# Folding the chunk inverse into the operand of a bidirectional RWKV-7 chain, with grams and transposes in 64x64 tiles

## The chip, the cores and the metric

The kernel runs on one core of one Trainium2 chip, as one program. The metric is the device time of one execution in microseconds, the median of three runs. A core has five engines that work from their own in-order queues: TensorE (PE; its weight loads are listed as PEld), VectorE (DVE), ScalarE (ACT), GpSimd (POOL) and SyncE (SP), which here only issues DMAs.

## The reference: what is computed

Two layers of a token mixer run over 256 context tokens and 1024 latent tokens of width 1024. Each layer projects its input once, and the columns go to three groups of heads: A, a bidirectional RWKV-7 recurrence (6 heads of 64); B, grouped-query attention; C, neighbourhood attention on a grid. Each group is gated, all are concatenated, projected and normalised. The change lies in A, whose recurrence is, for each token and each direction:

```
def _rwkv7_step(S, inp):
    r, w, k, v, kk, b = inp
    sa = einsum('bhvk,bhk->bhv', S, kk)
    S = S * w[:, :, None, :] - sa[..., None] * b[:, :, None, :] + v[..., None] * k[:, :, None, :]
    return S, einsum('bhvk,bhk->bhv', S, r)
```

The state S is 64x64 per head. It is carried from the context into the latent tokens, once forwards and once backwards, and the two outputs are added.

## The kernel before, in words

`layer_proj` (L182) makes the projections. Its last part and the whole of `attention` (L831: the heads of B and C, two PSUM banks for `st`, two for `sm`, one for `y`) are written after the recurrent part `rwkv` (L516) but run beside it: the program is built under a planner (`schedule_with_timeline_sim=True`), which puts each engine's instructions in an order by program order and by its own estimate of when each is ready. So each queue holds a mixture of recurrent work and attention work, in a fixed order. `out_proj` (L1144) follows when attention and the recurrent part have written their gated outputs.

The recurrent part cuts the 1280 tokens into 10 waves of 128 tokens, and a wave into 4 steps of 32 tokens. Both directions (d) and the six heads (three columns c, two halves p) go together. Within a step the recurrence is a linear system in blocks of 32 tokens: the sums `sa` of all 32 tokens come from the inverse of a triangular 32x32 matrix times a right side.

A wave has these stages, each a function that gives instructions:

- `wave_pre` (L555, letter p) loads r, kk, kd and bd by DMA, makes the decays and the scaled operands. It writes `kb` (the scaled keys) and half of the operand tile `G`; L593 clears the other half of each block of G on GpSimd. There are six G tiles, two for each of three waves.
- `wave_gram` (L612, g) multiplies `kb` with G on TensorE (L620: full 128 rows, 64 columns at a time) and writes the masked products into the cleared halves of G (L625, VectorE, sixteen instructions of 64x192 per wave).
- `wave_low` (L600, l) sends the 16x16 diagonal blocks of the matrix through DRAM into a layout for inversion.
- `wave_inv` (L641, i) inverts the 16x16 blocks on VectorE (L653, L655) and sends the result through DRAM back into `di`.
- `wave_kt` (L628, k) transposes `kb` on TensorE (L635: 128x128 transposes) and copies it into the tiles `S` (L639, ScalarE, sixteen copies per wave).
- `wave_merge` (L673, m) joins the 16x16 inverses to 32x32 ones with two rounds of 32x32 products (L684). The first is masked on VectorE (L687), the second gives `tt` (L689).

`wave_chain` (L692) then runs four steps one after the other. A step has these instructions, each dependent on the one before:

- L706 loads v into the tile `X` (three X tiles in turn, `NX = 3`) and L708 clears its sa rows, on SyncE and GpSimd;
- L713: twelve products of G with X give the right side `rs` in PSUM;
- L716: ScalarE copies it to SBUF as `rsb`;
- L724: twelve 32x32 products of `tt` with `rsb` give `sa`;
- L730: four copies put `sa` into X (three on ScalarE, one on VectorE);
- L734: twelve products of S with X give the new state, which L739 (VectorE) scales into the next X.

The step's output products (`out_step`, L754, tile `py`) are kept back in the list `pend` and given after the next step's L716, in the middle of its chain.

The stages are called in the order "ikpglm" after each wave's chain: stages i, k and m for the wave two ahead, p, g and l for the wave three ahead. `behind` (L550) holds two places of the later work behind an instruction of the chain. All PSUM tiles of the stages (psz, pcu, gt, kt, mg, py, pso) take turns in one pair of banks, the tag "pp" of the pool `pa` (L523, `bufs=2`); the chain has a bank of its own, `ch`.

## Time and profile before

| what | value |
|---|---|
| median of three runs | 2471.63 us (2459.14 to 2474.3) |
| the profiled execution, its time | 2478.63 us |
| its span in the trace | 2476.9 us, 57781 instructions |
| mean granted TensorE clock | 0.937 |
| DMA | 298.17 MB, mean 120 GB/s |

How to read the lines shown in the prediction. In a group line stand the line of the code, engine, operation, tile written and tiles read (out<-in), shapes and types with the count of records; then the busy time in microseconds and the mean of one in nanoseconds; then the idle time of the engine just before, and what ended it. For TensorE the tiling stands as rows*columns of the weights. An f32 product gives two records, a transpose one. A tile view gives minimum, median and maximum duration in ns and the start of the first and last record. In a timeline stand start and length in us and, with xN, how many like instructions are merged in the line. In the view by stretches stand for each stretch its length, busy time and count for PE, PEld, DVE, ACT and POOL, then the granted clock, the share of DMA and GB/s; restricted to one line of code, only its engines are listed. A busy PE is not a PE at its peak: the time that a product needs to run through the array is counted as busy.

### The profile page before, as it was taken

How to read it: one execution, taken by the hardware profiler on the slowest of the kernel's cores; microseconds unless marked ns; L12 is line 12 of the kernel's file. 1: busy time of each engine (PE TensorE's matmuls, PEld its weight loads, DVE VectorE, ACT ScalarE, POOL GpSimd, SP SyncE). 2: the span in 40 equal slices, each digit the busy share in tenths (PEclk: the TensorE clock that was granted, in tenths of full speed). 3: DMA queues.
4: the chain of work that ended last, by engine and by line, in shares of the span. 5: the costliest groups of instructions: out<-in, count | busy, mean ns of one | idle time of the engine just before them, and what ended most of it. 6: DMA issues, size and time to landing. Idle time of an engine off the chain costs nothing.

```text
span 2476.9 us, 57781 instructions
## 1 busy us (share of the span) xinstructions
PE 2189.6 (88%) x22616; PEld 1645.0 (66%) x22616; DVE 1625.1 (66%) x3063; ACT 1003.5 (41%) x2186; POOL 1184.1 (48%) x1438
## 2 busy tenths in 40 slices
PE   6989999987888888989899999899868788989697
PEld 3777898765555555545897777787645555556397
DVE  5686423545768777775396785525468688778646
ACT  3333413334445454463233434223345444445522
POOL 4464426335555554462245456434456545545433
PEclk9999999996879999998999999999879999999899
DMA  7344335446555444351332445334555545332522
GB/s 281 112 162 164 111 92 123 120 108 139 126 116 136 114 100 119 102 177 34 101 103 91 146 161 182 107 90 121 141 116 140 102 99 117 84 90 64 161 71 94
DMA packets 448241, 298.17 MB, mean 120 GB/s; under 512 B 249600, under 2 KB 395880, under 8 KB 446944
## 3 DMA queue, kind: packets, MB, share of 16 engines
q1 hardware_dynamic: 439936, 281.71, 41.6%
q0 software_dynamic: 7392, 10.28, 1.5%
q8 instruction: 178, 2.92, 0.5%
q10 hardware_dynamic: 640, 2.49, 0.4%
q14 instruction: 95, 0.78, 0.1%
HBM read 198.37 MB, written 91.79 MB: 117 GB/s over the span
## 4 chain that ended last, share of the span: by engine, by line
PE 44%; DVE 21%; DMA 15%; issue 7%; ACT 6%; POOL 4%; SPq 3%; DVEq 0%; POOLq 0%; ACTq 0%
PE pj L203 5%; PE pj L204 5%; PE pj L205 5%; PE y L948 4%; DMA yf<-yg_d 3%; PE st L963 3%; PE sm L894 3%; DMA ls_d<-G 3%; DVE G L625 2%; PE st L964 2%; DVE mx L896 2%; DVE tmp L653 2%; PE ch L734 2%; PE py L754 1%; DMA lin<-ls_d 1%
## 5 line engine op out<-in xcount | busy, mean ns | idle before, releaser
L204 PE MATMUL pj<-hlo,wh 128*128 128x512 f32 (+1 forms) x1072 | 401.4, 375 | 14.3 <-DVE hlo L480 8.0
L203 PE MATMUL pj<-hhi,wh 128*128 128x512 f32 (+1 forms) x1072 | 403.2, 378 | 9.4 <-ACT qr L348 5.2
L205 PE MATMUL pj<-hhi,wl 128*128 128x512 f32 (+1 forms) x1072 | 400.6, 374 | 0.2 <-POOL wl L169 0.2
L204 PEld LDWEIGHTS pj<-hlo,wh 128*128 128x128 f32 x1072 | 205.0, 191 | 56.2 <-DVE hlo L480 8.3
L203 PEld LDWEIGHTS pj<-hhi,wh 128*128 128x128 f32 x1072 | 204.4, 191 | 54.8 <-issue 6.8
L169 POOL TENSOR_TENSOR wl<-wf,wh 128x512 fp32r<-128x512 f32 x104 | 143.8, 1387 | 202.2 <-ACT wh L168 178.7
L896 DVE TENSOR_REDUCE mx<-sm 128x1 f32<-128x512 f32 (+1 forms) x372 | 198.8, 554 | 50.1 <-PE sm L894 47.6
L205 PEld LDWEIGHTS pj<-hhi,wl 128*128 128x128 f32 x1072 | 204.9, 191 | 38.4 <-issue 3.3
L970 ACT ACTIVATE pt<-st 128x512 f32<-128x512 f32 (+1 forms) x292 | 164.9, 583 | 130.1 <-PE st L964 122.8
L948 PE MATMUL y<-pt,v 128*64 128x256 f32 (+1 forms) x1392 | 211.5, 398 | 2.3 <-ACT pt L973 1.4
L894 PE MATMUL sm<-k,q 128*128 128x256 f32 (+2 forms) x436 | 166.1, 422 | 25.8 <-DVE mx L896 19.5
L963 PE MATMUL st<-q,k 128*128 128x512 f32 (+3 forms) x376 | 165.0, 444 | 21.1 <-DVE rc L1012 5.9
L1186 PE MATMUL pj<-yh,wh 128*128 128x256 f32 x576 | 160.2, 290 | 24.4 <-ACT yh L1160 23.1
L1187 PE MATMUL pj<-yl,wh 128*128 128x256 f32 x576 | 164.0, 288 | 0.8 <-POOL yl L1161 0.8
L1188 PE MATMUL pj<-yh,wl 128*128 128x256 f32 x576 | 162.2, 286 | 0.0
L977 POOL TENSOR_TENSOR acc<-acc,pt 128x512 f32<-128x512 f32 x80 | 106.4, 1330 | 102.7 <-ACT pt L970 101.4
L948 PEld LDWEIGHTS y<-pt,v 128*64 128x64 f32 x1392 | 94.0, 142 | 89.6 <-issue 58.0
L964 PE MATMUL st<-q,k 65*128 65x512 f32 (+3 forms) x376 | 146.7, 393 | 1.9 <-ACT q L908 1.2
L894 PEld LDWEIGHTS sm<-k,q 128*128 128x128 f32 x436 | 80.6, 201 | 89.8 <-DVE mx L896 37.0
L625 DVE TENSOR_TENSOR G<-gt,msk 64x192 f32<-64x192 f32 (+1 forms) x320 | 110.5, 345 | 39.7 <-PE gt L620 28.4
L708 POOL MEMSET X<- 32x192 f32 x320 | 81.2, 254 | 102.0 <-PE py L754 74.6
L1186 PEld LDWEIGHTS pj<-yh,wh 128*128 128x128 f32 x576 | 109.9, 196 | 26.0 <-ACT yh L1160 23.5
(276 smaller groups left out, 5104.5 us busy)
## 6 DMA issues: line engine op xcount, KB each, us to landing
wf<-win SPq DMA_DIRECT2D x104, 256.0 KB
wm<-wmod SPq DMA_DIRECT2D x32, 512.0 KB
yf<-yg_d SPq DMA_DIRECT2D x72, 128.0 KB
wt<-wm SPq DMA_DIRECT2D x8, 1024.0 KB
gate_d<-o SPq DMA_DIRECT2D x32, 256.0 KB
wf<-wout SPq DMA_DIRECT2D x16, 512.0 KB
ldkk<-rw_d SPq DMA_DIRECT2D x40, 192.0 KB
ldkd<-rw_d SPq DMA_DIRECT2D x40, 192.0 KB
```

The lines of the kernel that those rows point to most:

```text
L203: nc.tensor.matmul(out=ps[:, :n], lhsT=wh, rhs=hhi[:, k, t0:t0 + n], start=(k == 0), stop=False)
L204: nc.tensor.matmul(out=ps[:, :n], lhsT=wh, rhs=hlo[:, k, t0:t0 + n], start=False, stop=False)
L205: nc.tensor.matmul(out=ps[:, :n], lhsT=wl, rhs=hhi[:, k, t0:t0 + n], start=False, stop=(k == KT - 1))
L894: nc.tensor.matmul(out=sp_[:, :o], lhsT=q[0][:, qc:qc + 128], rhs=k[0][:, c0:c0 + o], start=True, stop=True)
L896: nc.vector.tensor_reduce(out=mx[:, n_:n_ + 1], in_=sp_[:, :o], op=ALU.max, axis=AX.X)
L948: mm = nc.tensor.matmul(out=y[64 * i:64 * i + 64, a0:a1], lhsT=v[:, t, :], rhs=pt[:, p0:p0 + a1 - a0], start=start, stop=stop and at == le ...
L963: nc.tensor.matmul(out=o, lhsT=k[0][:, 128 * t:128 * t + 128], rhs=q[0][:, qa:qb], start=True, stop=False)
L964: mm = nc.tensor.matmul(out=o, lhsT=k[1][0:65, 128 * t:128 * t + 128], rhs=q[1][0:65, qa:qb], start=False, stop=True)
L970: nc.scalar.activation(out=pt[:, :w], in_=sp_[:, :w], func=AF.Exp)
L1186: nc.tensor.matmul(out=p_, lhsT=wh[m][:, k], rhs=yh, start=(x_ == 0), stop=False)
L1187: nc.tensor.matmul(out=p_, lhsT=wh[m][:, k], rhs=yl, start=False, stop=False)
L1188: nc.tensor.matmul(out=p_, lhsT=wl[m][:, k], rhs=yh, start=False, stop=(x_ == KT - 1))
```

## The change

- In the chain, L716 (the copy `rsb`) and L724 (the products with `tt`) are gone; the products of L713 write `sa` directly. The output products in `pend` now stand between them and the copies into X.
- `wave_merge` keeps its first round; the mask `omk` has changed its sign, and `tt` is not made.
- A new stage `wave_fold` (letter f, called last, for the wave two ahead) finishes the inverse in PSUM by accumulation, copies it negated into a block-diagonal tile `bd`, transposes the first halves of the G operand by products with the identity, multiplies them with `bd`, and writes the result back over them. Its PSUM tiles come from the same pair of banks.
- `wave_gram` takes the two halves p as separate 64x64 products instead of one 128-row product with zeros in it, so that G needs no clearing (L593 is gone), and the masking takes eight instructions of 64x384 instead of sixteen of 64x192.
- `wave_kt` transposes by 64x64 products with the identity, and copies with eight instructions of 64x384 instead of sixteen of 64x192.

The core of the diff, without the renaming of `rs` and the sign of `omk`:

```diff
+        bd = rp.tile([128, 6, 4, 32], F32, tag="bd", name="bd")
+        nc.gpsimd.memset(bd, 0.0)
...
-                    nc.gpsimd.memset(g[64 - 64 * p:128 - 64 * p, :, :, p, 0:64 if need_r else 32], 0.0)
...
-                            nc.tensor.matmul(out=gt[64 * i:64 * i + 64, c, :, :nr], lhsT=kb[:, c, 2 * h + i, :], rhs=g[:, 2 * h + i, c, :, :nr],
-                                             start=True, stop=True, tile_position=(0, 64 * i))
+                            for p in range(2):
+                                rs_, os_ = slice(64 * p, 64 * p + 64), slice(64 - 64 * p, 128 - 64 * p)
+                                nc.tensor.matmul(out=gt[os_, i, c, :nr], lhsT=kb[rs_, c, 2 * h + i, :], rhs=g[rs_, 2 * h + i, c, p, :nr],
+                                                 start=True, stop=True, tile_position=(64 * p, 64 - 64 * p))
...
-                        nc.tensor.transpose(kt[:, c, :], kb[:, c, 2 * h:2 * h + 2, :].rearrange("q j f -> q (j f)"), ident)
+                                nc.tensor.matmul(out=kt[os_, i, c, :], lhsT=kb[rs_, c, 2 * h + i, :], rhs=ident[rs_, rs_],
+                                                 start=True, stop=True, tile_position=(64 * p, 64 - 64 * p))
...
+        def wave_fold(w):
+
+            gs, di = prep[w]["g"], prep[w]["di"]
+            for hf in range(2):
+                mg = pa.tile([128, 2, 3, 32], F32, tag="pp", name="mi")
+                for j in range(2):
+                    for c in range(3):
+                        for lhs in (None, di):
+                            for d in range(2):
+                                for p in range(2):
+                                    q = QSA[d][p]
+                                    nc.tensor.matmul(out=mg[q:q + 32, j, c, :], lhsT=ident[q:q + 32, q:q + 32] if lhs is None else lhs[q:q + 32, 0, 2 * hf + j, c, :],
+                                                     rhs=di[q:q + 32, 1, 2 * hf + j, c, :], start=lhs is None, stop=lhs is not None, tile_position=(q, q))
+                for d in range(2):
+                    for p in range(2):
+                        q = QSA[d][p]
+                        nc.scalar.activation(out=bd[q:q + 32, :, 2 * d + p, :], in_=mg[q:q + 32].rearrange("q j c t -> q (j c) t"), func=AF.Copy, scale=-1.0)
+                for j in range(2):
+                    tr = pa.tile([128, 3, 128], F32, tag="pp", name="tr")
+                    for c in range(3):
+                        for d in range(2):
+                            for p in range(2):
+                                q = QSA[d][p]
+                                nc.tensor.matmul(out=tr[q:q + 32, c, :], lhsT=gs[d][:, 2 * hf + j, c, p, 0:32], rhs=ident, start=True, stop=True, tile_position=(0, q))
+                    gT = r2.tile([128, 3, 128], F32, tag="gT", name="gT")
+                    nc.scalar.copy(gT, tr)
+                    gp = pa.tile([128, 3, 2, 2, 32], F32, tag="pp", name="gp")
+                    for c in range(3):
+                        nc.tensor.matmul(out=gp[:, c].rearrange("q d p t -> q (d p t)"), lhsT=gT[:, c], rhs=bd[:, 3 * j + c].rearrange("q b t -> q (b t)"), start=True, stop=True)
+                    for d in range(2):
+                        nc.scalar.copy(gs[d][:, 2 * hf + j, :, :, 0:32], gp[:, :, d])
...
-                            nc.tensor.matmul(out=rs[q:q + 32, c, :], lhsT=gs[d][:, jc[d], c, p, 0:32], rhs=x[:, d, c, p, :],
+                            nc.tensor.matmul(out=sa[q:q + 32, c, :], lhsT=gs[d][:, jc[d], c, p, 0:32], rhs=x[:, d, c, p, :],
                                              start=True, stop=True, tile_position=(0, q))
-                rsb = r2.tile([128, 3, 64], F32, tag="rsb", name="rsb")
-                nc.scalar.copy(rsb, rs)
                 for f in pend:
                     f()
                 pend.clear()
-                for c in range(3):
-                    for d in range(2):
-                        for p in range(2):
-                            q = QSA[d][p]
-                            nc.tensor.matmul(out=sa[q:q + 32, c, :], lhsT=tt[q:q + 32, jc[d], c, :], rhs=rsb[q:q + 32, c, :],
-                                             start=True, stop=True, tile_position=(q, q))
...
-            for c in "ikpglm":
-                v = w + (2 if c in "ikm" else 3)
+            for c in "ikpglmf":
+                v = w + (2 if c in "ikmf" else 3)
```

More of the change, by code (lines that the diff above doesn't have):

```diff
@@ L524, in rwkv @@
         bank = pb.tile([128, 512], F32, tag="ch", name="ch")
-        rs = sa = bank[:, 0:192].rearrange("p (c v) -> p c v", c=3)
+        sa = bank[:, 0:192].rearrange("p (c v) -> p c v", c=3)
         z = bank[:, 0:384].rearrange("p (d c v) -> p d c v", d=2, c=3)
@@ L719, in wave_chain @@
                 pend.clear()
-                for c in range(3):
-                    for d in range(2):
-                        for p in range(2):
-                            q = QSA[d][p]
-                            nc.tensor.matmul(out=sa[q:q + 32, c, :], lhsT=tt[q:q + 32, jc[d], c, :], rhs=rsb[q:q + 32, c, :],
-                                             start=True, stop=True, tile_position=(q, q))
                 for d in range(2):
@@ L806, in out_block @@
             nc.sync.dma_start(out=yg_d[0:3, :, ts_].rearrange("c p t -> p c t"), in_=ybc)
-        stages = dict(p=wave_pre, g=wave_gram, l=wave_low, i=wave_inv, k=wave_kt, m=wave_merge)
+        stages = dict(p=wave_pre, g=wave_gram, l=wave_low, i=wave_inv, k=wave_kt, m=wave_merge, f=wave_fold)
         waiting, loaded = [], []
@@ L1379, in arrays @@
     of, ob = (ii >= 16) & (t < 16), (ii < 16) & (t >= 16)
-    o["omk"] = f(np.concatenate([ob, of, ob, of], 0).astype(np.float32))
+    o["omk"] = f(-np.concatenate([ob, of, ob, of], 0).astype(np.float32))
     rpb = np.asarray(inp["na_rpb"])
```

39 lines of the change are left out of this document (18 added, 21 removed).

## The prediction

> **What bounds the kernel now.** I read the page first, then busy time by stretch, then the timeline of single steps, then groups by line.
>
> ```profile
> PE 2189.6 (88%) x22616; PEld 1645.0 (66%) x22616; DVE 1625.1 (66%) x3063; ACT 1003.5 (41%) x2186; POOL 1184.1 (48%) x1438
> PE 44%; DVE 21%; DMA 15%; issue 7%; ACT 6%; POOL 4%; SPq 3%; DVEq 0%; POOLq 0%; ACTq 0%
> ```
>
> No engine ends the kernel alone: TensorE has 44% of the chain that ended last, VectorE 21%, DMA 15%. In each layer the recurrent part (waves and chain) shares the core with the attention heads. The next view is by stretch: two with chain and attention together, then the products L948 of attention alone in the same two stretches, each followed by the stretch after the last chain step.
>
> ```profile
> 842.00:1060.00 218.00, 197.23 (x3039) 124.47 (x3040) 161.49 (x366) 110.41 (x272) 112.73 (x145) 0.95 0.43 109
> 2040.00:2300.00 260.00, 235.60 (x3545) 147.88 (x3535) 210.06 (x454) 130.14 (x308) 137.49 (x174) 0.96 0.37 89
> ...
> 842.00:1060.00 218.00, 41.59 (x264) 17.77 (x264) 0.95 0.43 109
> 1060.00:1190.00 130.00, 37.57 (x256) 17.05 (x256) 0.92 0.33 100
> ...
> 2040.00:2300.00 260.00, 56.25 (x368) 24.41 (x368) 0.96 0.37 89
> 2300.00:2342.00 42.00, 13.43 (x96) 6.08 (x96) 0.97 0.51 156
> ```
>
> In both layers attention, not the chain, comes to its end last: it still runs 130 us after the chain in the first layer and 42 us in the second. Beside the chain it issues 264/218 = 1.21 and 368/260 = 1.42 products per us, alone 256/130 = 1.97 and 96/42 = 2.29. The ratios are 0.61 and 0.62. So a microsecond taken off the recurrent part leaves 0.615 of a microsecond of attention work to be done later, and the end comes only **0.385 us** earlier. That is the exchange rate I use for everything that shortens or lengthens a wave.
>
> Now one chain step and the start of the next, from the timeline (start, us, engine, line):
>
> ```profile
> 2242.26 0.63 PE L713 MATMUL ch<-X,G 128*32 128x64 f32 x24
> 2245.17 0.30 ACT L716 COPY rsb<-ch 128x192 f32<-128x192 f32 x1
> 2245.66 0.54 PE L724 MATMUL ch<-rsb,tt 32*32 32x64 f32 x24
> 2246.48 0.98 ACT L730 COPY X<-ch 32x192 f32<-32x192 f32 x3
> 2249.95 0.34 DVE L730 COPY X<-ch 32x192 f32<-32x192 f32 x1
> 2251.33 0.87 PE L734 MATMUL ch<-X,S 128*64 128x64 f32 x24
> 2253.71 1.12 DVE L739 TENSOR_TENSOR X<-ch,dc 64x384 f32<-64x384 f32 x2
> 2255.35 0.54 PE L713 MATMUL ch<-X,G 128*32 128x64 f32 x24
> 2255.96 0.32 ACT L716 COPY rsb<-ch 128x192 f32<-128x192 f32 x1 [0.62 <-PE ch L713]
> 2258.44 0.54 PE L724 MATMUL ch<-rsb,tt 32*32 32x64 f32 x24
> ```
>
> The step takes 13.1 us, of which its own instructions are under 5 us. The rest is queueing in in-order engines behind attention and the preparation of later waves. From the end of L713 to the end of L724 it is 2246.20 - 2242.89 = 3.3 us, and in the next step 2258.98 - 2255.89 = 3.1 us. That piece is what the change deletes: **3.2 us a step**.
>
> Next the preparation of a wave against the chain that needs it. The first row groups seven waves; the others are wave 5 of the first layer.
>
> ```profile
> L689 DVE TENSOR_TENSOR tt<-mg,di x7: 547/550/558, 636.2 to 986.7; 128x384 f32<-128x384 f32 x7
> ...
> 720.31 0.49 PE L635 MATMUL kt<-c_ident,kb 128*128 128x128 f32 x3
> 721.18 0.54 PE L713 MATMUL ch<-X,G 128*32 128x64 f32 x24
> 726.94 2.60 ACT L639 COPY S<-kt 64x192 f32<-64x192 f32 x8
> ...
> 757.46 1.03 PE L684 MATMUL mg<-di,G 32*32 32x32 f32 x96
> 762.09 0.54 DVE L687 TENSOR_TENSOR di<-mg,omk 128x384 f32<-128x384 f32 x1
> 763.58 1.02 PE L684 MATMUL mg<-di 32*32 32x32 f32 x96
> 765.69 0.55 DVE L689 TENSOR_TENSOR tt<-mg,di 128x384 f32<-128x384 f32 x1
> 784.64 0.30 PE L713 MATMUL ch<-X,G 128*32 128x64 f32 x4
> ```
>
> A wave takes (986.7 - 636.2)/6 = 58.4 us, 14.6 us a step. The chain of wave 4 starts at 721.18; wave 5's inverse (tt) is ready at 766.24 and its chain starts at 784.64. So the inverse now has 18.4 us to spare. This slack is what the new stage must fit in.
>
> **The change part by part.** Rows for the prices:
>
> ```profile
> L625 DVE TENSOR_TENSOR G<-gt,msk 64x192 f32<-64x192 f32 (+1 forms) x320 | 110.5, 345 | 39.7 <-PE gt L620 28.4 <-POOL G L594 4.9 <-PE ch L734 0.7
> L639 ACT COPY S<-kt 64x192 f32<-64x192 f32 x320 | 100.1, 313 | 33.9 <-PE kt L635 20.8 <-PE ch L734 8.6
> L739 DVE TENSOR_TENSOR X<-ch,dc 64x384 f32<-64x384 f32 x156 | 86.2, 552 | 26.7 <-PE ch L734 24.9 <-PE py L754 0.3
> L730 ACT COPY X<-ch 32x192 f32<-32x192 f32 x240 | 74.4, 310 | 51.5 <-PE ch L724 47.3
> L593 POOL MEMSET G<- 64x768 f32 (+1 forms) x80 | 57.0, 712 | 35.5 <-PE py L754 25.4 <-PE ch L713 3.5 <-issue 3.0
> L756 ACT COPY yst<-py 128x192 f32<-128x192 f32 x72 | 22.4, 317 | 83.1 <-PE py L754 75.6 <-DMA go<-gate_d 1.9 <-DMA ls_d<-G 1.6
> L582 ACT ACTIVATE lp<-pcu 128x384 f32<-128x384 f32 x40 | 19.6, 491 | 38.1 <-PE pcu L577 27.8 <-POOL G L596 7.0 <-POOL wl L169 1.7
> ...
> 752.21 1.53 PE L620 MATMUL gt<-G,kb 128*64 128x128 f32 x24
> ...
> 847.60 0.94 PE L577 MATMUL pcu<-tri,th 128*128 128x128 f32 x6
> ```
>
> A product in f32 is two records. The burst of 4 L713 records at 784.64 takes 0.30 us and that of 24 takes 0.54, so a burst has some 0.2 us of fill. Without it the time per record is: L713 and L724 14 ns, L734 28 ns, L684 8.7 ns, L620 55 ns.
>
> *Work per wave (20 waves).* TensorE: four L724 bursts go, -1.4 us. The merge loses one of two sets of 96 records and gains two (identity, then the correction): +0.8. The grams become 96 records of 64 columns for 48 of 128: at L734's 28 ns (two side by side) 2.7 us for 2.6. The transposes become 96 records for 12 of 128 columns: 2.7 for 1.3, +1.4. The new transposes of G: 96 records of 128 columns through 32-wide tiles, twice L713's 14 ns: +2.7. The new full products: 24 records at 2 x 55 ns: +2.6. Together +6.1 us. ScalarE: rsb copies 4 x 0.318 = -1.3; S copies 16 x 0.313 become 8 of 64x384 at 0.49 (nearest row L582), -1.1; the fold 8 x 0.31 + 4 x 0.49 + 8 x 0.317 = +7.0. Together +4.6. VectorE: masks 16 x 0.345 become 8 x 0.552 (L739), -1.1, and tt -0.55. GpSimd: four clears of G, -2.85. SyncE issues the same DMAs. The clear of the new operand bd is once per layer, about 0.7 us, behind the clear of X and ahead of the first wave; its cover is the projections, and without it the cost is 0.7 us per layer.
>
> Side by side is not shown for 64x64 tiles in the trace. Bounds: 28 ns as taken, or 56 ns one after the other, +5.4 us per wave on TensorE. I take 28 because L684, whose four row groups write one bank, gets 96 records of 32 columns through in 1.02 us where one after the other (half of 56 ns each) would be 2.7. The Trainium skill, TensorEngine Tiling (Array Packing), section Restrictions and Gotchas, speaks against it: row tiles are said not to be able to use the same PSUM bank at the same time, and both new forms write their two row tiles to one bank. By that rule grams and transposes cost the upper bound; the L684 row disagrees with the rule for 32x32 tiles, and no row here shows 64x64.
>
> *The path.* The chain itself loses 4 x 3.2 = 12.8 us a wave: 58.4 becomes 45.6. But now the first product of a wave needs the folded operand, since step 0 uses block 0 of one direction and block 3, the last folded, of the other. The fold starts where the correction of the merge is ready (762.63), some 3 us earlier than now, because the clears, masks and S copies ahead of it are cheaper by 2.85, 1.1 and 1.1 us and lie partly beside one another (bounds 0 and 5). Its serial length without overlap is, per half: products 1.0, four copies 1.24, then twice (transposes 0.9, copy 0.49, products 0.94, two copies 0.64), 8.2; two halves 16.4, or 12.8 if the transposes lie beside the copies. What queueing adds, I take from the S stage, which has the same pattern of product, ScalarE copy and two PSUM buffers: 4 x (0.49 + 1.25) = 7.0 us of work took 729.54 - 720.31 = 9.2, a factor of 1.3. So 17 to 22 us, taken 19. Ready at 759.6 + 19 = 778.6, against 784.64 now: a wave comes **6 us** earlier, set by the fold and no longer by the chain. Break-even is a fold of 25 us. Queued behind the fold in the two PSUM buffers of this part are the output products L754, on which the clear and reload of X wait.
>
> The first wave of a layer has no slack:
>
> ```profile
> L724 PE MATMUL ch<-rsb,tt x1920: 214/214/312, 460.2 to 2291.4; 32*32 32x64 f32 x192
> L689 DVE TENSOR_TENSOR tt<-mg,di x20: 544/551/558, 458.8 to 2221.0; 128x384 f32<-128x384 f32 x20
> ```
>
> The first inverse is made at 458.8 and used at 460.2. There the fold of 19 us stands in place of the second half of the merge (766.24 - 763.58 = 2.7 us) and the 3.2 us of the removed piece: some **13 us** later per layer.
>
> *Sum.* 18 waves (all but each layer's first) x 6.0 = 108 us of recurrent part, x 0.385 = -42; the two late starts 2 x 13 x 0.385 = +10; together -32. The extra work of the other engines is taken as covered by TensorE's idle 10% beside the chain (218 - 197 and 260 - 236 us, 5.5 us per wave) and by the drop on VectorE and GpSimd; if that cover fails, see the second rival. The profiled execution took 2478.6 us, so 2447; it was 7 us above the median of 2471.6 (2459.1 to 2474.3), so the forecast for the median is **2440 us**.
>
> **The rivals.** (1) *The fold is hidden*: the transposes of G need only the gram, and the planner may put them early; the chain then sets the wave, 12.8 x 18 x 0.385 = -89, with the late starts -79, **2393**. For it: 18.4 us of slack. Against: the merge already comes right behind the next wave's grams.
>
> (2) *TensorE takes the gain back*: its 5.5 us of idle time per wave are less than the 6.1 us added, so a wave stays at 58.4 + 0.6 us; 18 x 0.6 x 0.385 = +4, with the late starts +14, **2486**, no change. For it: 90% busy. Against: that share counts the 0.2 us fill of each burst.
>
> (3) *Slower, by the fold itself*: ten more PSUM tiles per wave pass through two buffers. The merge shows how such a stage can stretch: 1.03 + 0.54 + 1.02 + 0.55 = 3.1 us of work took 766.24 - 757.46 = 8.8, a factor of 2.8, and this row of what L754 waited for shows that the chain's output stalls on it (us, times):
>
> ```profile
>   DVE tt L689: 39.1, 16
> ```
>
> At 2.8 the fold is 41 us. From 25 us it decides; halfway, at 33, a wave is 8 us longer: 18 x 8 x 0.385 = +55, with the late starts +65, **2537**. Against: the fold is drained by ScalarE, half busy, not by VectorE.
>
> (4) *The 64x64 tiles do not run side by side* (the rule above): +5.4 us ahead of the fold eats the 6 us, and 20 x 5.4 = 108 us of TensorE work at 0.385 add 42; -4 + 42 + 10 = +48, **2520**. Here the change does not do what it says.
>
> **How the numbers follow.** Forecast 0.42, rival 1 0.19, rival 2 0.17, rival 3 0.16, rival 4 0.06. About 1% is what a measurement of this kernel can tell from no change. Faster by more: 0.27 of the forecast's 0.42 and all of rival 1, 0.46. Within 1%: 0.14 of the forecast and 0.13 of rival 2, 0.27. Slower: 0.01 of the forecast, 0.04 of rival 2 and all of rivals 3 and 4, 0.27. The forecast's own range, for a fold of 17 to 22 us and 0 to 5 us of cheaper preparation, is 2412 to 2482. The range reaches from 2380, below rival 1, to 2525, above rival 4 and into rival 3; most of rival 3 and the lowest part of rival 1 are left out.
>
> **What would show it.** Right: no L724 nor rsb rows; a step near 13 us, with ScalarE's copies of X starting about 1 us after L713's end; the wave near 52 us; the fold's last copy just ahead of the next wave's first L713 product; a longer stretch of attention alone at the end of each layer. Bursts of the new grams near 28 ns a record mean side by side, 56 ns rival 4. Wrong: a wave at 58 us with TensorE over 95% busy (rival 2), a wave over 60 us whose first L713 waits for a fold copy (rival 3), or attention's rate beside the chain far from 1.2 to 1.4 products per us, which would break the exchange rate.

## The result, and the profile after

The changed kernel takes 2620.05 us (median of four runs, 2615.03 to 2632.47) against 2468.15 us for the kernel before on the same chip (2459.14 to 2474.3): a ratio of 1.0626, with a 95% interval of 1.0574 to 1.0678. The forecast of 2440 us was wrong in size and in sign, and the time lies above the range. The profiled execution took 2632.47 us, with a span of 2630.7 us. Of the times below, those of e3 and e4 leave out one execution each, which took 5295 and 7125 us; with it the median of e3 is 2490.83 us, the 2491 us of the expectations.

First the busy times on the page of the changed kernel:

```profile
PE 2338.0 (89%) x27656; PEld 1793.8 (68%) x27656; DVE 1580.8 (60%) x2883; ACT 1083.8 (41%) x2346; POOL 1127.1 (43%) x1360
```

TensorE is busy 2338.0 - 2189.6 = 148.4 us longer than before, and the span is 2630.7 - 2476.9 = 153.8 us longer. VectorE and GpSimd have less to do, as foreseen.

Next the four steps of one chain, wave 4 of the first layer, in its timeline (start, us, engine, line). The first two rows are the starts of step 0 and step 1; L755 copies the sums into X right behind L746. The third row starts step 2. The rows from 872.65 on are what happens until step 3.

```profile
801.34 0.54 PE L746 MATMUL ch<-X,G 128*32 128x64 f32 x24
...
814.58 0.87 PE L746 MATMUL ch<-X,G 128*32 128x64 f32 x24
815.51 0.96 ACT L755 COPY X<-ch 32x192 f32<-32x192 f32 x3 [7.73 <-PE ch L746]
...
823.93 0.78 PE L746 MATMUL ch<-X,G 128*32 128x64 f32 x24
...
872.65 0.94 PE L721 MATMUL gp<-bd,gT 128*128 128x128 f32 x6
873.51 0.54 PE L779 MATMUL py<-X,G 128*32 128x64 f32 x24
873.62 0.54 ACT L723 COPY G<-gp 128x192 f32<-128x192 f32 x2 [1.28 <-PE gp L721]
874.16 1.14 DVE L764 TENSOR_TENSOR X<-ch,dc 64x384 f32<-64x384 f32 x2 [0.61 <-PE py L779]
874.16 1.17 POOL L741 MEMSET X<- 32x192 f32 x4 [1.16 <-PE py L779]
...
877.68 0.22 PE L746 MATMUL ch<-X,G 128*32 128x64 f32 x1 [1.39 <-DMA X<-vt_d]
...
891.31 0.54 PE L746 MATMUL ch<-X,G 128*32 128x64 f32 x24
```

The hop that was deleted is gone: the copies start 815.51 - 815.45 = 0.06 us after L746's end here, where it was 3.3 us and the second product. Steps 0 and 1 take 13.2 and 9.4 us. But from step 2 to step 3 (called the third step from here on) it is 877.68 - 823.93 = 53.8 us. The kernel before has the same long step, but only of 17 to 25 us in waves 1 to 4. The reader is to see the order in those rows. L721 is the last product of the fold of wave 5, the *next* wave. Only then comes L779, the output product of step 0 of wave 4, for its PSUM tile takes its turn behind the fold's ten tiles in the two buffers. L764 wants to write the X of step 3, which is the X of step 0 (three X tiles take turns), and waits for L779; the clear L741 and the load of X too; step 3 comes last. Then wave 5 starts at 891.31, 17 us after its folded operand was ready (L723 ends at 874.16). L746 of the first steps of waves 3 to 7 starts at 722.8, 801.3, 891.3, 966.5 and 1036.4, so a wave takes (1036.4 - 722.8) / 4 = 78 us where it took 58.4; over the layer's ten waves, the last of which has no fold behind it, it is (1186.8 - 467.3) / 10 = 72, by the first and last start of L746 (row in e1 below).

The list of waits sums up the same one (us, times, longest):

```profile
POOL X L741 <- PE py L779: 96.2, 35, 15.9
```

In the second layer attention has no stretch alone any more, where one longer than 42 us was forecast; over both layers the first and last start of its products and of the chain's:

```profile
L973 PE MATMUL y<-pt,v x1392: 272/379/690, 592.2 to 2465.9; 128*64 128x256 f32 x173, 128*64 128x128 f32 x26
L759 PE MATMUL ch<-X,S x1920: 219/222/369, 497.9 to 2468.3; 128*64 128x64 f32 x192
```

The new 64x64 products run side by side. Twenty-four records of the gram take 0.91 us; less the fill of 0.2 us that is 30 ns for one:

```profile
825.30 0.91 PE L625 MATMUL gt<-G,kb 64*64 64x64 f32 x24
```

Last, the dearest new costs on TensorE, by line (records, then busy us and mean ns of one, then idle time before):

```profile
L721 PE MATMUL gp<-bd,gT 128*128 128x128 f32 x480 | 78.4, 305 | 14.0 <-ACT gT L718 14.0
L716 PE MATMUL tr<-c_ident,G 128*32 128x128 f32 x1920 | 76.1, 295 | 11.2 <-ACT G L723 10.5 <-issue 0.6
L642 PE MATMUL kt<-c_ident,kb 64*64 64x64 f32 x1920 | 74.8, 226 | 9.2 <-ACT G L723 5.6 <-ACT S L646 3.6
L625 PE MATMUL gt<-G,kb 64*64 64x64 f32 (+1 forms) x1920 | 71.5, 225 | 3.5 <-POOL kb L591 2.7 <-ACT iv L586 0.8
```

and of the kernel before, the rows that they replace or that fall away:

```profile
L620 PE MATMUL gt<-G,kb 128*64 128x128 f32 (+1 forms) x960 | 67.8, 286 | 5.9 <-ACT iv L583 3.0 <-POOL kb L588 2.8
L724 PE MATMUL ch<-rsb,tt 32*32 32x64 f32 x1920 | 47.4, 229 | 2.1 <-ACT rsb L716 2.0
L635 PE MATMUL kt<-c_ident,kb 128*128 128x128 f32 x240 | 44.8, 300 | 10.4 <-DVE tt L689 7.3 <-ACT S L639 3.2
```

### The profile page after: what moved, and what is told of

Its sections match the earlier page's. It is cut to its first block, busy times and chain, and to the rows that moved or that the text cites. A ratio compares the mean times of both kernels' runs of the same rounds, so it can differ in the third digit from the quotient of the medians.

```text
span 2630.7 us, 67863 instructions
## 1 busy us (share of the span) xinstructions
PE 2338.0 (89%) x27656; PEld 1793.8 (68%) x27656; DVE 1580.8 (60%) x2883; ACT 1083.8 (41%) x2346; POOL 1127.1 (43%) x1360
## 4 chain that ended last, share of the span: by engine, by line
PE 21%; DVE 10%; DMA 9%; issue 3%; ACT 3%; POOL 2%; SPq 2%; DVEq 0%; POOLq 0%; ACTq 0%
DMA ls_d<-G 2%; PE y L973 2%; PE pj L1212 1%; PE pj L1213 1%; PE pj L204 1%; PE pj L203 1%; PE pj L1211 1%; PE pj L205 1%; DMA stg<-q_d 1%; DMA lin<-ls_d 1%; PE st L988 1%; DVE G L629 1%; PE sm L919 1%; PE kt L642 1%; PE gp L721 1%
## 5 line engine op out<-in xcount | busy, mean ns | idle before, releaser
L919 PE MATMUL sm<-k,q 128*128 128x256 f32 (+2 forms) x436 | 155.8, 411 | 20.6 <-DVE mx L923 11.1
L741 POOL MEMSET X<- 32x192 f32 x320 | 81.8, 256 | 125.4 <-PE py L779 96.2
L1002 DVE TENSOR_TENSOR acc<-acc,pt 128x512 f32<-128x512 f32 x112 | 112.2, 1009 | 36.8 <-ACT pt L995 36.0
```

The lines of the kernel that those rows point to most:

```text
L919: nc.tensor.matmul(out=sp_[:, :o], lhsT=q[0][:, qc:qc + 128], rhs=k[0][:, c0:c0 + o], start=True, stop=True)
L1002: eng.tensor_tensor(out=acc[i][:, :w], in0=sums[i][:, :w], in1=pt[:, :w], op=ALU.add)
```

## The experiments

Four theories were to be told apart.

- **A**, the first: the long third step, because the output products stand behind the next wave's fold, lengthens the waves and so the time.
- **B**: TensorE's own time decides; what is added to it is paid, whoever waits.
- **C**: the chain waits for the folded operand itself.
- **D**: the pass of a wave through the two PSUM buffers decides, with all its tiles, and TensorE's idle tenth covers added work.

### The third step made free (A)

e1: the output products leave the two buffers.

```diff
-            y = pa.tile([128, 3, 64], F32, tag="pp", name="py")
+            y = bank[:, 192:384].rearrange("p (c v) -> p c v", c=3)
```

> The changed kernel, but the output products py are written to columns 192 to 384 of the chain's own bank, so they no longer take a turn in the two PSUM buffers pp. Theory A (in the pp order the output products of a wave stand behind the next wave's fold, and step 3 of the chain, which needs the X that step 0's output products still read, waits for them): the third step interval falls from 37 to 54 us to 20 us or less, a wave from 71 to 56 to 62 us, and the time from 2620 to about 2460 us (2400 to 2520). Theory B (the added TensorE and ScalarE work sets the wave): that work is all still there, so 2620 us within 1%, third step unchanged. Theory C (the chain waits for the folded operand itself): the fold stays where it is, so first steps of waves wait for it as now and the time stays within 1 to 2% of 2620 us.

Measured: 2623.86 us, ratio 1.0603 (1.0567 to 1.0639). The timeline of one chain of this kernel, step 0 (in two parts), step 2 and step 3:

```profile
892.90 0.43 PE L746 MATMUL ch<-X,G 128*32 128x64 f32 x4
...
907.50 0.53 PE L746 MATMUL ch<-X,G 128*32 128x64 f32 x20
...
923.03 0.54 PE L746 MATMUL ch<-X,G 128*32 128x64 f32 x24
933.86 0.54 PE L746 MATMUL ch<-X,G 128*32 128x64 f32 x24
```

The third step is 10.8 us, as theory A said, and the time has not moved. So the mechanism is real and it isn't the price, at least not alone. The wave is shorter, but not the 56 to 62 us of theory A: the starts of waves 0 and 9 give (1080.5 - 470.3) / 9 = 67.8 us, for (1153.8 - 467.3) / 9 = 76.3 in the change. The first two rows say why. Only four records of step 0 run at 892.90; the other twenty, which need the block that is folded last, come 14.6 us later, behind the last L721 of the fold (at 901.86 in the same timeline). With the third step free, the wait of theory C appears at the first step, in each of the waves 0 to 8.

In the first layer the rows of the chain's first product and of attention's products (first and last start), in the kernel before, the changed kernel and e1, show where the time went:

```profile
L713 PE MATMUL ch<-X,G x960: 216/219/316, 400.1 to 1054.1; 128*32 128x64 f32 x192
L948 PE MATMUL y<-pt,v x736: 272/379/689, 588.0 to 1182.3; 128*64 128x256 f32 x154, 128*64 128x128 f32 x30
```

```profile
L746 PE MATMUL ch<-X,G x960: 216/219/316, 467.3 to 1186.8; 128*32 128x64 f32 x192
L973 PE MATMUL y<-pt,v x736: 272/379/690, 592.2 to 1237.2; 128*64 128x256 f32 x152, 128*64 128x128 f32 x32
```

```profile
L746 PE MATMUL ch<-X,G x960: 216/219/316, 470.3 to 1107.1; 128*32 128x64 f32 x192
L973 PE MATMUL y<-pt,v x736: 272/379/690, 623.8 to 1261.4; 128*64 128x256 f32 x153, 128*64 128x128 f32 x31
```

From the change to e1 the chain ends 80 us earlier, and attention, which begins 32 us later, ends 24 us later. What the chain gained, attention lost.

e4: the fold in four quarters, each behind a step of the chain.

```diff
+                if w > 0 and w + 1 < NW:
+                    fold_part(w + 1, j // 2, j % 2)
                 if yst is not None:
                     pend.append(lambda j=j, x=x, jc=jc: out_step(w, j, x, jc, gs, yst))
```

> The changed kernel, but the fold of the next wave is given in four quarters, one behind each step of the chain, so that each output product stands behind one quarter of the fold and not behind all of it. Theory A: step 3 waits for one quarter (about 6 us) and not for 25 us; the third step falls to about 15 to 20 us, a wave to 58 to 62 us, the time to about 2460 us (2400 to 2530). Theory B: 2620 us within 1%. Theory C: the fold ends later against its chain, so 2620 us or more.

Measured: 2631.34 us, 1.0661 (1.0621 to 1.0702). A misses again. Of this run only the time is used.

e2: six X tiles.

```diff
-        NX = 3
+        NX = 6
```

> The changed kernel with six X tiles for three (NX = 6), nothing else. Theory A: the output products still stand behind the fold, but no step of a wave waits for the X of its own wave; the third step interval falls to about 10 to 15 us, a wave to about 60 to 65 us (the output products then run as a burst of some 5 us behind the fold, not over 13 us), the time to 2480 us (2430 to 2550). Theory B: 2620 us within 1%. Theory C: 2620 us within 1 to 2%, the wait only moves to the first step of the next wave, which then grows by the 30 to 40 us that the third loses.

Measured: 3140.69 us, 1.2699 (1.267 to 1.2728), which no theory expected. The row of attention's products (first and last start) in two kernels of below, e12 and then e15:

```profile
L974 PE MATMUL y<-pt,v x1392: 272/379/690, 1196.3 to 3092.0; 128*64 128x256 f32 x172, 128*64 128x128 f32 x27
```

```profile
L973 PE MATMUL y<-pt,v x1392: 272/379/690, 612.6 to 2457.4; 128*64 128x256 f32 x172, 128*64 128x128 f32 x27
```

By the same row attention starts in e2 at 1154.2 us, after the last step of the chain (957 us), and not at 592. The X tiles take 9 KB more of each partition of SBUF. e12 takes 3 KB more and starts attention as late; e15 does the same work with no new tile and starts it at 613. So e2 and e12 show what it costs when attention begins only after the recurrent part, and nothing on A or C. That attention finds no room in SBUF beside it fits the sizes, but no run shows what attention waited for.

### The parts of the change by themselves

e3: no fold, so the chain multiplies with the unfolded operand; the rest of the change stays.

```diff
-                if 0 <= v < NW:
+                if 0 <= v < NW and c != "f":
                     stages[c](v)
```

> The changed kernel without the stage fold: the chain multiplies with the unfolded operand, so the inverse is left out of the computation (the correction's second half, the transposes of G, the products with the inverse and their copies). It gives the price of the whole stage. Theory A: with the fold out of the pp order the wave falls by the fold's length of 25 us and more, to 44 to 50 us, attention ends last again, and the time is 2380 to 2430 us (the first rival of the prediction gave 2393). Theory B: only TensorE's 5.3 us and ScalarE's 7 us of work per wave go, so a wave of 64 to 66 us and 2500 to 2540 us. Theory C: 2380 to 2450 us too, so this run does not tell A from C.

Measured: 2486.21 us, 1.0072 (1.0047 to 1.0098). The fold costs 134 us, but without it nothing is won. Neither theory has that: A expected 2380 to 2430, B some 2520.

e14: as e3, with the old grams, clears and transposes as well (the diff of those two stages and of L593 undone). It is the shortened chain alone.

> The shortened chain alone, on the old tiles and without the fold (the inverse is left out of the computation). It is what the change has to win with, free of its costs. Theory B: TensorE loses the products with the inverse and the second set of the merge, 62 us, so about 2410 us. The first rival of the prediction: 12.8 us a wave off the chain, 2393 us. Theory D (the turns of the buffers set the waves): four waits fewer do little, and only the second tile of the merge goes, 2440 us or more.

Measured: 2422.62 us, 0.9802 (0.9772 to 0.9832), 49 us less. Between B (2410) and D (2440). This is what the shortened chain is worth free of its costs. Part of it no whole version can have: here no first step waits for an inverse, and the first state product of the first layer starts 469.3 - 418.6 = 50.7 us earlier (rows of L734 and L755, shown with the exchange rate below).

e13: fold and shortened chain with the old tiles.

> The fold and the shortened chain alone: the changed kernel with the old grams, clears and transposes. The parts measured so far, each on another base, are +73 us for the new tiles, -57 us for the shortened chain (2491 against 2548) and +129 us for the fold (2620 against 2491). If they add up: 2620 - 73 = 2547 us. Theory B (work of TensorE alone): only the 34 to 40 us of work of the new tiles go, about 2580 us.

Measured: 2569.51 us, 1.0389 (1.0359 to 1.0419). The parts don't add up exactly (2547 expected), and B's 2580 is nearer. On the old tiles the fold costs 2569.51 - 2422.62 = 147 us, with 129.9 us more of TensorE's busy time.

e6: the new grams and transposes alone, in the kernel before. Its edit is the two stages `wave_gram` and `wave_kt` of the change, without L593.

> The kernel before with the grams and transposes of the changed kernel alone (64x64 tiles, no clearing of G, eight masks for sixteen, eight copies for sixteen); the merge, the chain and the inverse as before. Theory B: TensorE's time grows by 30 us in the transposes and 4 in the grams (by the two pages), so about 2500 us (2490 to 2510) though VectorE, ScalarE and GpSimd are relieved of 5 us a wave. Theory D: the pass through the buffers is some 5 us shorter, 18 x 5 x 0.385 = 35 us less, about 2436 us.

Measured: 2547.72 us, 1.0304 (1.0273 to 1.0335). Slower, against D; 73 us on its chip's 2474.79, more than twice what B expected.

e7: the changed kernel with the old stage k.

> The changed kernel with the old stage k: 128x128 transposes, and sixteen copies of 64x192 for eight of 64x384. Theory B: TensorE gives 30 us back, so about 2590 us (2580 to 2600), though ScalarE gets more to do. Theory D: the copies make the pass through the buffers longer by 1 to 2 us a wave, so 2620 to 2640 us.

Measured: 2593.51 us, 1.0483 (1.0446 to 1.0521), 27 us less than the changed kernel. TensorE's rows kt say 30. B.

e11: the new grams alone in the kernel before. e16: the same, with the clear put back.

```diff
                     gv = g[rs_, :, :, p, :].rearrange("q j c f -> q c j f")
+                    nc.gpsimd.memset(g[64 - 64 * p:128 - 64 * p, :, :, p, 0:64 if need_r else 32], 0.0)
```

> The kernel before with the grams of the changed kernel alone (64x64 tiles, no clearing of G, eight masks for sixteen); transposes as before. Grams and transposes together cost 73 us. Theory B: the grams add 4 us to TensorE, so 2475 to 2485 us, and the transposes have the rest. If the relief of GpSimd and VectorE (4 us a wave) or the order that the planner makes of it counts, then clearly off that: below 2455 us by theory D, or 2500 us and more if it is the order.

> The kernel before with the 64x64 grams and the eight masks, but with the clearing of G on GpSimd put back though nothing needs it. The grams without clearing took 2518 us. If the cheaper GpSimd moved other work into a worse order, the time falls back to 2475 to 2485 us; if it is the 64x64 products themselves, it stays at 2510 to 2525 us.

Measured: 2518.22 us, 1.0192 (1.0161 to 1.0223), and 2521.01 us, 1.02 (1.0174 to 1.0225). So the grams alone cost 47 us, and the missing clear has no part in it: it is the 64x64 products or their wider masks, which no run separates. B, with 4 to 14 us, and D, with a gain, both miss. The row of the gram in e11:

```profile
L622 PE MATMUL gt<-G,kb 64*64 64x64 f32 (+1 forms) x1920 | 74.8, 231 | 15.1 <-ACT iv L583 7.0 <-POOL kb L588 3.8 <-POOL G L593 2.8
```

The gram's own busy time grew by 7 us. But the granted clock of TensorE is 0.919 to 0.923 in all four executions, against 0.930 to 0.938 in the seven of the kernel before on the same chip. 0.935 / 0.921 is 1.5%, 33 us of TensorE's 2190 us; the profile's page has TensorE busy 2226.7 - 2189.6 = 37.1 us longer. Here the lower clock goes with the longer time, but it does not belong to 64x64 grams as such: the change, which has them too, ran at 0.936 to 0.946, and e8 (next), which has none, at 0.918 to 0.930. What sets it is not shown.

e8: the kernel before with the edit of e1.

> The kernel before, with the output products written to columns 192 to 384 of the chain's own bank, so that they leave the two PSUM buffers pp: the same products and copies, fewer waits. Theory B: only the fill that a burst shares with its neighbour is saved, 0 to 15 us, so 2455 to 2471 us. Theory D: the pass through the buffers loses four tiles and the third step its wait, 5 us a wave and more, so 2435 us or less.

Measured: 2486.1 us, 1.0071 (1.004 to 1.0101). Not D: the tiles that leave the two buffers bring nothing. B's 2455 to 2471 us are missed too, by 15 us and more.

### Work without waits, waits without work

e5: TensorE work that nobody reads or waits for, in the kernel before.

```diff
+        def extra():
+            for _ in range(8):
+                nc.tensor.matmul(out=bank[:, 384:512], lhsT=ident, rhs=ident, start=True, stop=True)
...
                     stages[c](v)
+                    if c in "ikgl":
+                        extra()
```

> The kernel before, with products added that nobody reads and nobody waits for: after each of the stages i, k, g and l eight 128x128 products of the identity with itself into columns 384 to 512 of the chain's bank, which nothing else uses. 80 bursts of 16 records at 110 ns and a fill of 0.2 us are some 155 us of TensorE's time, as much as the change added (148 us by the two pages). Theory B (TensorE's own time sets the two layers, so that work added to it is paid in full and waits taken from the chain are worth nothing): 2471 + 130 to 160, 2600 to 2630 us. Theory D (the pass of a wave through the two PSUM buffers sets the waves, and TensorE's idle tenth covers added work): these products hold no buffer, so at most 2530 us.

Measured: 2569.86 us, 1.0403 (1.0373 to 1.0434). The page:

```profile
PE 2336.5 (91%) x23896; PEld 1795.9 (70%) x23896; DVE 1607.5 (62%) x3063; ACT 1008.7 (39%) x2186; POOL 1187.7 (46%) x1438
```

TensorE is busy 2336.5 - 2189.6 = 146.9 us longer, and the time is 95 us longer, though no instruction waits for the new work. So 95 / 146.9 = 0.65 of it is paid. B is too dear, D too cheap: the idle tenth covers a third of the work, not all of it.

e9: the same work in place of the fold (the edits of e3 and e5 together).

> The changed kernel without the fold (the inverse is left out of the computation, as in the run without the fold, 2491 us), and in its place the products of the identity that nobody waits for, 146 us of TensorE's time in the kernel before; the fold has about 150. Theory B (TensorE's time decides): 2491 + 98 (the price that the same products had in the kernel before) to + 147 us, 2589 to 2638 us. Theories C and D (the waits of the fold, for its operand or for its buffers, make the loss): TensorE has more room under the shortened chain, so at most 2550 us.

Measured: 2607.27 us, 1.0555 (1.0515 to 1.0596): 121 us more than e3, for 2334.5 - 2187.6 = 146.9 us more of TensorE's busy time. B: work of the fold's size costs nearly what the fold costs, 121 of 134 us, though nothing waits for it.

e10: a fold with all its tiles and waits, but fewer and narrower products and smaller copies. Of its three groups of products one is shown:

```diff
-                    for c in range(3):
-                        for d in range(2):
-                            for p in range(2):
-                                q = QSA[d][p]
-                                nc.tensor.matmul(out=tr[q:q + 32, c, :], lhsT=gs[d][:, 2 * hf + j, c, p, 0:32], rhs=ident, start=True, stop=True, tile_position=(0, q))
+                    nc.tensor.matmul(out=tr[:, 0, 0:32], lhsT=ident, rhs=gs[j][:, 2 * hf + j, 0, 0, 0:32], start=True, stop=True)
```

> The changed kernel with a fold that keeps its ten PSUM tiles, its order, its sixteen copies and the chain's wait for it, but has two to four records of 32 columns in each tile for 24 to 96 (so most of the inverse is left out of the computation). TensorE's part of the fold falls from some 9 us to some 2.5 us a wave. Theory B: 2491 + 20 x 2.5 x (0.66 to 1), 2524 to 2541 us. Theory D: the turns in the two buffers stay and only 6 us of the fold's 25 go, so the wave stays at 64 us or more and the time at 2580 us or more.

Measured: 2594.94 us, 1.051 (1.047 to 1.0551): 109 us more than e3. It is D's number, but B does not fall by it, for the thin fold is not thin in TensorE's time. Its rows (records, then busy us and mean ns of one):

```profile
L710 PE MATMUL gp<-bd,c_ident 128*128 128x32 f32 x160 | 38.7, 329 | 0.0
L705 PE MATMUL tr<-G,c_ident 128*128 128x32 f32 x160 | 36.4, 314 | 11.9 <-DVE di L691 11.3 <-ACT G L712 0.6
L709 PE MATMUL gp<-gT,c_ident 128*128 128x32 f32 x160 | 35.5, 309 | 1.9 <-DVE di L691 1.4 <-ACT gT L707 0.6
L698 PE MATMUL mi<-di,c_ident 128*128 128x32 f32 x80 | 18.1, 312 | 5.9 <-DVE G L629 4.7 <-DVE rc L1026 0.9 <-PE mg L689 0.2
```

These products of 32 columns come nearly alone, and a record takes some 0.3 us. Where the rows overlap counted once, the thin fold keeps TensorE busy 114.8 us, 5.7 us a wave; the expectation had 2.5. The whole fold has 202.1 us, 10.1 a wave. The profile's page agrees: TensorE is busy 2302.4 - 2187.6 = 114.8 us longer than in e3. With that, theory B's own formula gives 2491 + 114.8 x (0.66 to 1), 2567 to 2606 us, and the measured time lies in it. So e10 does not tell B from D. (The expectation also counts sixteen copies, where ScalarE's instructions give (2346 - 1946) / 20 = 20; and the tile gp has four narrow records for six wide ones, not for 24 to 96.)

e17 is e10 with the edit of e1.

> The thin fold (2595 us; most of the inverse left out of the computation) with the output products in the chain's own bank, so that no step of the chain waits for the turns of the fold any more. If the long third step is what the thin fold costs, the waits are gone and only its own TensorE work is left: 2491 + 33 to 50, 2525 to 2545 us. If the length of a wave's pass through the two buffers is what it costs, with or without the output products in it (theory D): 2580 us or more, with waves of 64 us and more.

Measured: 2536.16 us, 1.0267 (1.0233 to 1.0301): 59 us less than e10, and 50 more than e3. Steps 2 and 3 of one chain of e10, then of one of e17 (L735 is the first product of a step):

```profile
851.61 0.42 PE L735 MATMUL ch<-X,G 128*32 128x64 f32 x12
890.72 0.37 PE L735 MATMUL ch<-X,G 128*32 128x64 f32 x4
```

```profile
847.44 0.54 PE L735 MATMUL ch<-X,G 128*32 128x64 f32 x24
861.85 0.69 PE L735 MATMUL ch<-X,G 128*32 128x64 f32 x24 [0.57 <-DVE X L753]
```

The third step goes from 39.1 to 14.4 us and the time follows, while the fold's own TensorE work stays (113.8 us). So with the thin fold the wait of theory A, and what goes with it, is worth 59 us, and the pass through the buffers (D) is not the cost. Not all of the 59 us is idle time: TensorE is busy 2302.4 - 2269.8 = 32.6 us less, at a granted clock of 0.921 for 0.907.

e12 and e15: the whole fold, with its last copies written elsewhere, so that the chain doesn't wait for them. e12 writes to a new tile and says nothing on C (above); e15 writes to dead parts of `di`.

```diff
-                        nc.scalar.copy(gs[d][:, 2 * hf + j, :, :, 0:32], gp[:, :, d])
+                        nc.scalar.copy(di[:, :, 2 * hf + j].rearrange("p x c t -> p c x t"), gp[:, :, d])
```

> The changed kernel with the fold whole, but its last copies go to a tile that nobody reads, so the chain multiplies with the unfolded operand and never waits for the fold (the inverse is left out of the result). Theory B: all products are still there, 2620 us within 1%. Theory C (the chain waits for the folded operand): the wait is gone, so 2560 us or less. Theory D: the buffers are still taken in the same order, 2620 us too.

> As the run of the unused fold, but its last copies go to parts of the tile di that are no longer read, so that no room in SBUF is taken from attention (the inverse is left out of the result). All products, copies and turns in the buffers are kept; the chain does not wait for the fold. Theory C: 2560 us or less. Theories B and D: 2620 us within 1%.

Measured: e12 3224.13 us, 1.3037 (1.2991 to 1.3083); e15 2624.29 us, 1.0619 (1.0584 to 1.0654). In the change C's wait is not the cost by itself. In the timeline of e15 steps 1, 2 and 3 of one wave:

```profile
890.08 0.54 PE L746 MATMUL ch<-X,G 128*32 128x64 f32 x24
899.49 0.66 PE L746 MATMUL ch<-X,G 128*32 128x64 f32 x16
946.60 0.61 PE L746 MATMUL ch<-X,G 128*32 128x64 f32 x3
```

The third step is still 47 us long though the chain reads nothing of the fold. It is the turn in the buffers that it waits for, not the data. e1 takes out the one wait and e15 the other; no run takes out both and keeps the whole fold. The nearest is e9, with no wait and as much work, at 121 of the fold's 134 us.

e18: fold and shortened chain with the old tiles and the edit of e1, the best arrangement of the whole computation found here.

> Fold and shortened chain with the old grams and transposes (2570 us), and the output products in the chain's own bank: the whole computation, with the two dear parts that can be taken out of the change taken out. By the changed kernel, where that bank gave 4 us on 2620, and by the kernel before, where it cost 11: 2560 to 2580 us, still slower than before. If the waits were a cost beside TensorE's work: 2530 us or less.

Measured: 2542.54 us, 1.029 (1.0251 to 1.0329), 27 us less than e13: more than expected, and still 72 us above the kernel before. With the third step free, the fold still costs 2542.54 - 2422.62 = 120 us on the old tiles, for 107.8 us more of TensorE's busy time (e18 against e14), and 2623.86 - 2486.21 = 138 us on the new ones, for 131.9 (e1 against e3). No version found beats the kernel before, and e14 says why: with an inverse that costs nothing there are 49 us to win, while the fold alone adds 129.9 us to TensorE's busy time on the old tiles (e13 against e14).

## Why the prediction was wrong

The spans of the profiled executions, TensorE's busy time in them, and what is left:

| kernel | span, us | TensorE busy | rest |
|---|---|---|---|
| before | 2476.9 | 2189.6 | 287.3 |
| shortened chain alone (e14) | 2420.0 | 2149.5 | 270.5 |
| with the new tiles (e3) | 2480.4 | 2187.6 | 292.8 |
| with the fold, the change | 2630.7 | 2338.0 | 292.7 |
| the change, third step free (e1) | 2622.6 | 2319.5 | 303.1 |
| free work for the fold (e9) | 2603.7 | 2334.5 | 269.2 |
| fold and chain, old tiles (e13) | 2569.9 | 2279.4 | 290.5 |
| the same, third step free (e18) | 2541.2 | 2257.3 | 283.9 |
| before, with free work (e5) | 2574.5 | 2336.5 | 238.0 |
| thin fold (e10) | 2588.9 | 2302.4 | 286.5 |
| thin fold, third step free (e17) | 2530.3 | 2269.8 | 260.5 |

By the medians the parts are, one put on the other: chain -49, new tiles +64, fold +134. Their sum is the loss, 148 us on the first median of 2471.63. Put on in the other order, fold before tiles, they are -49, +147 and +51.

- **The step that failed** is this one: "The extra work of the other engines is taken as covered by TensorE's idle 10% beside the chain". It is not covered. Work that nobody waits for costs 0.65 of its length in the kernel before (e5) and 121 / 146.9 = 0.82 beside the shortened chain (e9). For the 148.4 us of the change that is 96 to 122 us of the loss. Rival 2 had the mechanism, but charged only what goes beyond the idle time, 0.6 us a wave.
- **The size of that work.** +6.1 us a wave were forecast; 148.4 / 20 = 7.4 were measured. By the rows: products gp 3.9 for 2.6 and transposes of G 3.8 for 2.7, where the fill of 0.2 us in each of their four bursts a wave, which the sum left out, explains 0.8 of the excess of each; the merge with the fold's end of the inverse +1.3 for +0.8 (L689 and L704 are busy 21.9 + 47.6 us, L684 was 44.3); transposes kt +1.5 for +1.4 and grams +0.2 for +0.1, right; the removed L724 -2.4 for -1.4.
- **The chain.** The removed piece was right: 3.2 us a step are gone. What it is worth was not: 12.8 us a wave, 89 us, by the first rival, and 49 as measured (e14). The waves of e14 show the step: from wave 1 to wave 9 of the first layer a wave takes 56.4 us for 60.5 before. The other three steps together are 9.2 us shorter, 3.1 each, but the third step is 5.1 us longer (23.7 for 18.6), since there the clear of X still waits for the output products (62.2 us in 24 waits over the run, 74.6 in 21 before).
- **The exchange rate** of 0.385. In the first layer the chain of the change ends 1186.8 - 1054.1 = 132.7 us later (last L746 and last L713 in the rows at e1), times 0.385 is 51, and attention ends 1237.2 - 1182.3 = 55 us later. That may be chance, for the added work on TensorE delays both. For the shortened chain it held in e14 and not in e3. The rows are those of attention's products and of the chain's, first and last start, in the kernel before, in e3 and in e14:

```profile
L948 PE MATMUL y<-pt,v x1392: 272/379/689, 588.0 to 2333.5; 128*64 128x256 f32 x174, 128*64 128x128 f32 x25
L734 PE MATMUL ch<-X,S x1920: 216/222/370, 469.3 to 2296.3; 128*64 128x64 f32 x192
```

```profile
L973 PE MATMUL y<-pt,v x1392: 272/379/690, 634.0 to 2351.9; 128*64 128x256 f32 x168, 128*64 128x128 f32 x31
L759 PE MATMUL ch<-X,S x1920: 219/222/370, 413.6 to 2209.0; 128*64 128x64 f32 x192
```

```profile
L969 PE MATMUL y<-pt,v x1392: 272/379/690, 591.9 to 2289.9; 128*64 128x256 f32 x173, 128*64 128x128 f32 x26
L755 PE MATMUL ch<-X,S x1920: 219/222/369, 418.6 to 2194.9; 128*64 128x64 f32 x192
```

  In e14 the last chain product comes 101 us earlier, times 0.385 is 39, and attention's last 44 us earlier. In e3 it comes 87 us earlier and attention's 18 us *later*; there attention begins 46 us later. Attention's place in the queues is fixed by the planner, which may put a chain that it takes for faster ahead of it. That the rate differs is shown; that the planner's order is the cause is only argued.
- **The fold and the wave.** The forecast had a wave set by the fold, whose last copy stands "just ahead of the next wave's first L713 product". It does not: in seven of the first layer's ten waves it ends 13 to 18 us before, and it is longer (23 to 31 us for 19, and 38 in the first wave). What waits is the third step of the *present* wave. The prediction named it in one sentence, "Queued behind the fold in the two PSUM buffers of this part are the output products L754, on which the clear and reload of X wait", and gave it no price in the wave. With three X tiles the fourth step of the chain needs it.
- **What that wait costs** depends on what else bounds. With the thin fold 59 us (e10 to e17), with the whole fold and the old tiles 27 (e13 to e18), in the change itself nothing that can be measured (e1 against the change), where the first step then waits for the fold. Work and wait overlap: as much work without any wait costs 121 us on e3 (e9), and the whole fold with both waits 134.
- **Rival 3** had the side right and the row right (what L754 waits for), but the wrong victim: it let the next wave wait for the fold (e15: that wait is worth nothing while the third step is held; e1: it comes back when the third step is free). Its 2537 us were still too low.
- **Rival 4** fell as put: 30 ns a record, not 56. Yet the tiles are dear: 2620 - 2570 = 51 us of the change (27 the transposes, e7; 47 the grams when alone, e11). For the transposes TensorE's 30 us explain it. For the grams alone the granted clock was lower (e11), in the change it was not, and the cause stays open.
- **The late starts** were too cheap. In the first layer the second step starts 26 us later, not 13; here it is in the changed kernel, then in the kernel before:

```profile
488.20 0.54 ACT L723 COPY G<-gp 128x192 f32<-128x192 f32 x2 [1.89 <-PE gp L721]
493.88 0.53 PE L746 MATMUL ch<-X,G 128*32 128x64 f32 x20
503.77 0.31 PE L746 MATMUL ch<-X,G 128*32 128x64 f32 x4
```

```profile
477.32 0.31 PE L713 MATMUL ch<-X,G 128*32 128x64 f32 x6
```

  e15, where the first steps don't wait for the fold, takes as long as the change. So this too is not what decides by itself.

## What to carry to other kernels

Where an engine is 90% busy in a stretch that two streams of work share, charge work added to it at two thirds of its length or more (0.65 and 0.82 here), and don't call it covered; a wait removed from the shorter stream was worth anything from nothing to 59 us here, since the next wait can take its place. A stage that takes turns in a rotating pool of buffers stands ahead of everything later in program order: follow each of those later tiles through every other ring (here three X tiles) to see which instruction of the critical chain needs it, and when. Count what a stripped stage still costs before reading a run by it: products that come nearly alone kept TensorE busy 114.8 us in the thin fold, for 202.1 in the whole one. If a change has a gain part and a cost part, run the gain part alone first: it bounds what any version can win.

## What the runs showed of the hardware

- 64x64 products whose two row tiles write to one PSUM bank run side by side: 30 ns a record (L625 above), where one after the other would be 56 by the prediction's rows. The Trainium skill, TensorEngine Tiling (Array Packing), section Restrictions and Gotchas, says that different row tiles can't use one bank at the same time; this trace disagrees.
- The mean granted clock of TensorE depends on the kernel, repeatably: 0.919 to 0.923 with the 64x64 grams in the kernel before (e11), 0.936 to 0.946 with them in the change, 0.898 to 0.907 with the thin fold (e10), 0.930 to 0.938 for the kernel before beside them, 0.939 to 0.951 with the free work (e5), and 0.859 to 0.868 in e2, where TensorE is busy 79% of the span. The Trainium skill, TensorE: Matmul & The Clock Gate, Part 1, says that a monitor lowers the clock when TensorE was not busy in a recent window. The runs e2 and e5 agree in direction; e10 and e11, no less busy (89%) than the kernel before (88%), are not explained by it.
- 3 KB more of each SBUF partition cost 600 us (e12 against e15): attention then begins at 1196 us, after the chain, and not at 613. That it is for want of room is inferred from the sizes.
- A product of 32 columns that comes nearly alone takes some 0.3 us a record (309 to 329 ns, e10), where 24 records in a burst take 0.54 us together (L735).
